# Half of the first weight sums in a Strassen-form down projection, moved from VectorE to a ScalarE copy and an adding transfer

## The chip, the cores and the metric

The kernel runs on one core of a Trainium2 chip, in one launch. The metric is device time in microseconds. A core has five engines with instruction queues of their own, each worked off in order: TensorE (PE in the profile; its weight loads are listed as PEld), VectorE (DVE), ScalarE (ACT), GpSimd (POOL) and SyncE (SP), which here only issues transfers. Sixteen DMA engines carry out the transfers of all queues.

## The reference

One layer of an encoder over 272 positions (16 learned meta tokens and 256 real ones), model width 2048, float32. Two attention groups share one input projection and one output projection; then comes a gated MLP of inner width 5632 with a residual. The part that matters here is its last line, the down projection:

```python
    return (jax.nn.silu(gc) * u) @ w_down      # (256, 5632) @ (5632, 2048), plus the residual h
```

## The kernel before

**Numbers.** Each float32 product is made of three products of a rounded type: every operand is split into a high part and a remainder (hi and lo), and hi x hi, hi x lo and lo x hi are summed in PSUM. For weights, ACT writes the high part (`whi`, listed at its helper's line L238) and DVE subtracts it from the weight to get the remainder (`wlo`, L242). There are four buffers of 1024 columns for whi and four for wlo, in turn. PE gives a pair of buffers back when it has used the piece.

**The down projection.** The 2048 output columns are cut in two. The upper 1024 are made as 8 tiles of 128 columns in the plain way (lines L1870 and L1871 for seven of them, L606 to L608 for the last). The first 1024 are made in the Strassen-Winograd form: with the 256 positions and the 1024 columns each cut in two, 7 block products take the place of 8. They are summed over 22 row pairs; a row pair g is 256 rows of the weight, two blocks of 128, and its four quarters of 128x512 stand side by side in one buffer of 2048 columns, `raw` = [B11 | B12 | B22 | B21] (in the profile `quarters<-in_w_down_s`, two transfers of 512 KB each). These products are at L278; their other operand is either an activation tile (`act`) or sums of activations that were saved to DRAM before and are loaded again (`sin<-s_down`).

The products need four sums of the quarters. `weight_sums` (L529) makes them on DVE in three subtractions, which are called T1, T2 and T3 below:

- T1, 1024 wide: [B12 - B11 | B22 - B12], at the listed L242 as `quarters<-quarters 128x1024`
- T2, 512 wide: B22 - (B12 - B11), and T3, 512 wide: T2's result minus B21, both `quarters<-quarters,quarters 128x512`

A row pair is used in four pieces, each split into whi and wlo like any weight: `raw` columns 1024 to 2047, `raw` columns 0 to 511, the two sums of T1, and the sums of T2 and T3. Pieces of the plain tiles (1024 or 512 columns) stand between them in a fixed order, which `work` (up to L479) writes down; PE takes all pieces in this order.

**Buffers.** There are two buffers of 2048 columns for `raw` (even pairs use one, odd pairs the other) and two for the sums (the same). A `raw` buffer goes back when both of its pieces have been split and T3 is done; then SP may load the pair after next into it.

**What sets the order.** The kernel is written as generator threads; each yields the engine and an assumed cost of its next instruction. The planner (`Flow`, L111) keeps a clock for each engine and always emits the instruction that could start first by these costs. What it emits is each engine's final order; on the chip an engine that must wait holds up all that stand behind it. A load (`load`, L483) is assumed to take its bytes at 350 per ns, in turn, plus 2000 ns. When a plain tile is complete, `down_out` (L1842) has ACT copy it out of PSUM, POOL do three steps on it (L266), and SP store it (`outT`).

Of the kernel before, what the change touches and what calls it, by code (L numbers as in the profile page):

```python
# [11 lines left out]
AF = mybir.ActivationFunctionType  # L12
ALU = mybir.AluOpType
# [192 lines left out]
def encoder_block(ctx: ExitStack, tc: tile.TileContext, io):  # L206
    nc = tc.nc
    ctx.enter_context(tc.manual_schedule())
    fl = Flow()
# [12 lines left out]
    def size(ap):  # L222
        n = 1
        for s in ap.shape[1:]:
            n *= s
        return n

    def in_psum(ap):
        return ap.tensor.name.startswith("bank")

    def columns(*scalars):
        return sum(not (s is None or isinstance(s, float)) for s in scalars)

    def ACT(out, in_, f, **kw):
        ns = (51 if in_psum(in_) else 93) + 0.833 * size(in_)
        ns += 93 * (columns(kw.get("scale")) + columns(kw.get("bias")) > 0)
        yield "act", ns + 113 * ("accum_out" in kw)
        nc.scalar.activation(out, in_, f, **kw)  # L238

    def TT(out, a, b, op):  # L240
        yield "dve", 68 + 1.04 * size(out)
        nc.vector.tensor_tensor(out, a, b, op)  # L242
# [54 lines left out]
    def one(slots):  # L297
        (t,) = yield slots, 1
        return t
# [141 lines left out]
    for w, f in enumerate(QUADS):  # L441
# [6 lines left out]
        for i in range(KC // 2):  # L448
            r = RowPair(io["w_up_s"][w][i], i, PW // 4)
# [18 lines left out]
    for g in range(FC // 2):  # L468
        r = RowPair(io["w_down_s"][g], g, PW // 2)
# [13 lines left out]
    def load(out, src, ev, queue):  # L483
# [4 lines left out]
        queue.dma_start(out, src)  # L488
        fl.set(ev, t + 2000.0 - fl.cur.t)

    n_loads = [0]

    def load_piece():
# [10 lines left out]
    def load_pair(r):  # L504
        if r.of == "up":
            r.raw, r.sums = yield raws, 2
        else:
            r.raw = yield from one(quarters)
        def load_S():
            if r.near:  # L510
                r.ev_S = ev_near[r.g]
                return
            r.S = yield from one(s_parts)
            src, saved = saved_sums[r.of][r.g]
            yield saved
            yield "sp", 600
            load(r.S, src, r.ev_S, nc.sync)

        if r.of == "up":
            yield from load_S()  # L520
        for a in range(0, 4 * r.q, PW):
            yield "sp", 600
            ev = r.loaded if a + PW == 4 * r.q else Event()
            load(r.raw[:, a : a + PW], r.src[:, a : a + PW], ev, nc.sync)
        if r.of == "down":
            yield from load_S()
        fl.spawn(weight_sums(r), (lambda: 0) if r.of == "up" else 2)

    def weight_sums(r):  # L529
        yield r.loaded  # L530
        if r.of == "down":
            r.sums = yield from one(sums4)
        t, raw, q = r.sums, r.raw, r.q
        yield from TT(t[:, : 2 * q], raw[:, q : 3 * q], raw[:, : 2 * q], ALU.subtract)
        fl.set(r.summed[0])
        yield from TT(t[:, 2 * q : 3 * q], raw[:, 2 * q : 3 * q], t[:, :q], ALU.subtract)
        yield from TT(t[:, 3 * q :], t[:, 2 * q : 3 * q], raw[:, 3 * q :], ALU.subtract)
        fl.set(r.summed[1])
        r.used("raw")
# [439 lines left out]
    for h in range(HEADS):  # L979
        t = apool.tile([P, 2, NT], F32R, name=f"ob{h}")  # L980
        ob.append((t[:, 0, :], t[:, 1, :]))
        t = apool.tile([P, 2, NT], F32R, name=f"oa{h}") if h < 6 else hl[KC - HEADS + h]
# [1228 lines left out]
```

## Time and profile before

| what | value |
|---|---|
| runs | 1108.64, 1108.89, 1109.74 us; median 1108.89 us |
| span of the profiled execution | 1106.7 us |
| PE busy in the span | 1100.6 us |
| DVE busy | 990.8 us |
| ACT busy | 735.1 us |
| POOL busy | 140.0 us |
| data moved by DMA | 239.41 MB |
| granted TensorE clock, whole span | 1.000 |

The profile comes from one execution; its own time is its span, from the first to the last instruction, and the runs are timed apart from it, start and end included. Busy shares are averages over stages that are limited by different things, so a stage is looked at by itself. PE's matmuls overlap, and their ends are modelled: how far two starts lie apart says more than how long one is listed. In a listing by groups a row gives line, engine, operation, output and inputs with their shapes and the count, then the total busy time and the mean of one in ns, then the idle time of the engine before these instructions and what ended it. In a timeline a row gives the start, the duration, and the instruction; rows of one kind that follow each other are merged with their count.

### The profile page before, as it was taken

What the parts mean: (1) busy time and instruction counts of PE and PEld (TensorE: products, weight loads), DVE (VectorE), ACT (ScalarE), POOL (GpSimd) and SP (SyncE); (2) the same over time, 40 slices, a digit from 0 to 9 for tenths busy, and PEclk for the clock granted to TensorE, in tenths of its full rate; (3) what the DMA queues carried; (4) which work ended last, traced back from release to release, by engine and by line L of the source; (5) the groups of instructions that cost most, each with busy time, mean ns of one, the idle gap of its engine ahead of it and who ended that gap; (6) DMA issues with size and microseconds to landing.
All of it is one profiled execution on the core that took longest, in us unless ns stands there. A gap on an engine that the chain in (4) does not pass through costs nothing.

```text
span 1106.7 us, 22544 instructions
## 1 busy us (share of the span) xinstructions
PE 1100.6 (99%) x8414; PEld 1061.8 (96%) x8414; DVE 990.8 (90%) x1837; ACT 735.1 (66%) x1470; POOL 140.0 (13%) x202
## 2 busy tenths in 40 slices
PE   9999999999999999999999999999999999999998
PEld 9999999999999999999999999999999988888888
DVE  8979888888878989999999999988988999999984
ACT  8788979798647776656666565665565565655663
POOL 3211222121433400000000000000000011100114
PEclk9999999999999999999999999999999999999999
DMA  9553434444665796657667577777688787777772
GB/s 323 199 172 124 148 127 151 139 163 134 230 188 161 207 343 229 198 181 243 224 193 230 179 248 241 238 229 244 203 275 299 260 299 250 251 258 266 281 249 77
DMA packets 72374, 239.41 MB, mean 216 GB/s; under 512 B 8136, under 2 KB 12744, under 8 KB 72264
## 3 DMA queue, kind: packets, MB, share of 16 engines
q1 hardware_dynamic: 71976, 237.69, 63.8%
q8 instruction: 66, 1.08, 0.4%
q14 instruction: 44, 0.36, 0.1%
q10 hardware_dynamic: 288, 0.27, 0.1%
HBM read 219.44 MB, written 17.83 MB: 214 GB/s over the span
## 4 chain that ended last, share of the span: by engine, by line
PE 90%; ACT 4%; DVE 3%; issue 1%; DMA 1%; POOL 0%; DVEq 0%; POOLq 0%; ACTq 0%
PE bank L278 24%; PE bank L606 18%; PE bank L607 18%; PE bank L608 18%; PE bank L1870 6%; PE bank L1871 3%; PE bank L284 2%; ACT whi L238 1%; ACT scr L238 1%; DVE wlo L242 1%; DVE scr L250 1%; DMA raw<-in_w_cq 1%; ACT qraw L238 0%; ACT bank L238 0%; DVE cols L258 0%
## 5 line engine op out<-in xcount | busy, mean ns | idle before, releaser
L238 ACT ACTIVATE whi<-raw 128x512 fp32r<-128x512 f32 (+2 forms) x479 | 358.1, 764 | 173.2 <-PE bank L607 83.5
L242 DVE TENSOR_TENSOR wlo<-raw,whi 128x512 fp32r<-128x512 f32 (+2 forms) x479 | 414.9, 885 | 43.2 <-ACT whi L238 42.1
L606 PE MATMUL bank<-hl,whi 128*128 128x258 f32 (+2 forms) x1528 | 438.5, 287 | 0.1
L607 PE MATMUL bank<-hl,whi 128*128 128x258 f32 (+2 forms) x1528 | 433.7, 284 | 0.0
L608 PE MATMUL bank<-hl,wlo 128*128 128x258 f32 (+2 forms) x1528 | 433.0, 283 | 0.2 <-DVE wlo L242 0.2
L608 PEld LDWEIGHTS bank<-hl,wlo 128*128 128x128 f32 x1528 | 290.1, 190 | 0.9 <-DVE wlo L242 0.7
L607 PEld LDWEIGHTS bank<-hl,whi 128*128 128x128 f32 x1528 | 289.6, 190 | 0.1
L606 PEld LDWEIGHTS bank<-hl,whi 128*128 128x128 f32 x1528 | 288.6, 189 | 0.5 <-ACT scr L238 0.3
L238 ACT ACTIVATE whi<-quarters 128x1024 fp32r<-128x1024 f32 x88 | 81.5, 950 | 64.8 <-PE bank L1870 46.0
L278 PE MATMUL bank<-whi,act 128*128 128x256 f32 (+1 forms) x420 | 111.5, 317 | 0.0
L1870 PE MATMUL bank<-act,whi 128*128 128x512 f32 x308 | 110.1, 397 | 0.0
L242 DVE TENSOR_TENSOR wlo<-quarters,whi 128x1024 fp32r<-128x1024 f32 x88 | 99.4, 1156 | 10.8 <-ACT whi L238 10.2
L266 POOL TENSOR_TENSOR mt<-mt,mt 128x256 f32<-128x256 f32 x7 | 6.8, 979 | 652.4 <-ACT mt L238 652.4
L1871 PE MATMUL bank<-act,wlo 128*128 128x256 f32 x308 | 86.4, 281 | 0.0
L278 PE MATMUL bank<-whi,sin 128*128 128x512 f32 (+1 forms) x272 | 83.5, 355 | 0.0
L278 PEld LDWEIGHTS bank<-whi,act 128*128 128x128 f32 x420 | 74.1, 189 | 5.7
L1870 PEld LDWEIGHTS bank<-act,whi 128*128 128x128 f32 x308 | 57.8, 188 | 13.9
L278 PE MATMUL bank<-whi,hl 128*128 128x256 f32 x288 | 66.5, 280 | 0.0
L278 PE MATMUL bank<-wlo,act 128*128 128x256 f32 (+1 forms) x210 | 66.3, 315 | 0.0
L238 ACT ACTIVATE whi<-more_raw 128x1024 fp32r<-128x1024 f32 (+2 forms) x46 | 44.1, 962 | 24.4 <-PE bank L607 9.9
L1871 PEld LDWEIGHTS bank<-act,wlo 128*128 128x128 f32 x308 | 58.1, 189 | 1.6
L278 PEld LDWEIGHTS bank<-whi,sin 128*128 128x128 f32 x272 | 49.5, 188 | 7.7
(278 smaller groups left out, 1947.9 us busy)
## 6 DMA issues: line engine op xcount, KB each, us to landing
raw<-in_w_gate SPq DMA_DIRECT2D x83, 512.0 KB, 5.0
raw<-in_w_in SPq DMA_DIRECT2D x52, 512.0 KB, 3.9
raw<-in_w_up_s SPq DMA_DIRECT2D x44, 512.0 KB, 4.9
quarters<-in_w_down_s SPq DMA_DIRECT2D x44, 512.0 KB, 6.9
raw<-in_w_up SPq DMA_DIRECT2D x34, 512.0 KB, 5.5
raw<-in_w_out SPq DMA_DIRECT2D x32, 512.0 KB, 4.0
raw<-in_w_down SPq DMA_DIRECT2D x32, 512.0 KB, 5.2
s_down<-sums SPq DMA_DIRECT2D x22, 512.0 KB, 4.1
```

The source lines that it names most:

```text
L238: nc.scalar.activation(out, in_, f, **kw)
L242: nc.vector.tensor_tensor(out, a, b, op)
L250: nc.vector.scalar_tensor_tensor(out, a, s, b, op0, op1)
L266: nc.gpsimd.tensor_tensor(out, a, b, op)
L278: nc.tensor.matmul(o, l, r, start=start, stop=stop)
L284: nc.tensor.transpose(o, i, ident[:n, :n])
L606: nc.tensor.matmul(ps, whi, xhi, start=start, stop=False)
L607: nc.tensor.matmul(ps, whi, xlo, start=False, stop=False)
L608: nc.tensor.matmul(ps, wlo, xhi, start=False, stop=stop)
L1870: nc.tensor.matmul(ps, whi, x, start=start, stop=False)
L1871: nc.tensor.matmul(ps[:, :n], wlo, x[:, 0, :], start=False, stop=stop)
```

## The change

In the row pairs with an odd number g, 11 of the 22, T1 is made in another way. ACT writes the negative of `raw` columns 0 to 1023 into the buffer of the sums. Then POOL issues a transfer of 128x1024 that adds `raw` columns 512 to 1535 to what stands there. For g = 1, 5, 9, ... the transfer reads its source from the `raw` buffer, for g = 3, 7, 11, ... from the weight in DRAM. T2 and T3 stay on DVE, and DVE waits for the landing ahead of T2. The planner assumes 1000 ns of POOL for the issue and 6000 ns from there to the landing.

```diff
+    def add_dma(out, src, ev):
+        yield "pool", 1000
+        nc.gpsimd.dma_start(out, src, accum_op=ALU.add)
+        fl.cur.t += 6000.0
+        fl.set(ev)
+
...
     def weight_sums(r):
...
         t, raw, q = r.sums, r.raw, r.q
-        yield from TT(t[:, : 2 * q], raw[:, q : 3 * q], raw[:, : 2 * q], ALU.subtract)
+        if r.of == "down" and r.g % 2:
+            yield from ACT(t[:, : 2 * q], raw[:, : 2 * q], AF.Copy, scale=-1.0)
+            src = raw if r.g % 4 == 1 else r.src
+            yield from add_dma(t[:, : 2 * q], src[:, q : 3 * q], Event())
+        else:
+            yield from TT(t[:, : 2 * q], raw[:, q : 3 * q], raw[:, : 2 * q], ALU.subtract)
         fl.set(r.summed[0])
         yield from TT(t[:, 2 * q : 3 * q], raw[:, 2 * q : 3 * q], t[:, :q], ALU.subtract)
         yield from TT(t[:, 3 * q :], t[:, 2 * q : 3 * q], raw[:, 3 * q :], ALU.subtract)
```

Here q is 512. The planner's new costs also move other instructions: the order of PE's instructions is the same in both kernels, DVE's and ACT's orders differ around the 11 pairs (T2 and T3 of an odd pair stand some steps later on DVE than before), POOL has 11 instructions more, and on SP one load and one store change places.

## The prediction

> **What bounds the kernel now.** I read the page first: the share of busy time, then the 40 slices.
>
> ```profile
> PE 1100.6 (99%) x8414; PEld 1061.8 (96%) x8414; DVE 990.8 (90%) x1837; ACT 735.1 (66%) x1470; POOL 140.0 (13%) x202
> ```
>
> PE looks full, but its ends are modelled, so a busy PE proves nothing by itself. The change lies in one stage, the down projection, the last fifth of the span. I therefore asked for a table of windows in that stage, and for its groups by line with the shapes kept apart.
>
> ```profile
> 880.00:900.00 20.00, 20.00 (x100) 16.75 (x99) 19.64 (x23) 14.18 (x19) 3.43 (x3) 1.00 0.70 253
> 1020.00:1040.00 20.00, 20.00 (x100) 16.75 (x99) 19.13 (x19) 13.26 (x16) 3.48 (x3) 1.00 0.88 308
> sum 200.00, PE 200.00 PEld 168.05 DVE 187.72 ACT 118.82 POOL 23.43; mean PE 20.00 PEld 16.81 DVE 18.77 ACT 11.88 POOL 2.34
> ...
> L1870 PE MATMUL bank<-act,whi 128*128 128x512 f32 x273 | 97.7, 397 | 0.0
> L1871 PE MATMUL bank<-act,wlo 128*128 128x256 f32 x273 | 76.6, 280 | 0.0
> L278 PE MATMUL bank<-whi,sin 128*128 128x512 f32 x171 | 60.7, 395 | 0.0
> L278 PE MATMUL bank<-whi,act 128*128 128x512 f32 x130 | 47.6, 394 | 0.0
> L278 PE MATMUL bank<-wlo,sin 128*128 128x512 f32 x85 | 33.4, 393 | 0.0
> L278 PE MATMUL bank<-wlo,act 128*128 128x512 f32 x65 | 25.3, 389 | 0.0
> ```
>
> The columns of a window are its length, then PE, PEld, DVE, ACT and POOL busy, the granted clock, the DMA share and GB/s. The clock is full. To see whether PE really runs without gaps I took the starts of neighbouring matmuls from the timeline:
>
> ```profile
> 904.78 0.40 PE L1870 MATMUL bank<-act,whi 128*128 128x512 f32 x1
> 905.01 0.28 PE L1871 MATMUL bank<-act,wlo 128*128 128x256 f32 x1
> 905.13 0.40 PE L1870 MATMUL bank<-act,whi 128*128 128x512 f32 x1
> ```
>
> A matmul of 512 columns is followed after 0.23 us, one of 256 after 0.12 us (0.232 and 0.118 as medians over the stage's 1213 matmuls). In the 200 us from 880 to 1080 there are 273+171+130+85+65 = 724 wide ones and 273 narrow ones: 724 x 0.232 + 273 x 0.118 = 200.2 us. That is the whole stretch. **PE has no gap in this stage**, so it sets the time; DVE, at 187.7 of 200 us, is close behind but not late. Two more rows say why DVE's load does no harm:
>
> ```profile
> L238 ACT ACTIVATE whi<-quarters 128x1024 fp32r<-128x1024 f32 x65 | 68.7, 1061 | 63.3 <-PE bank L1870 46.0 <-PE bank L278 11.5 <-issue 4.1
> L242 DVE TENSOR_TENSOR wlo<-quarters,whi 128x1024 fp32r<-128x1024 f32 x65 | 81.9, 1269 | 10.8 <-ACT whi L238 10.2
> ```
>
> ACT stands idle until PE frees one of the four whi buffers, DVE until ACT has filled one. Both are held back by PE, not PE by them.
>
> **The change part by part.** In the 11 odd row pairs T1 (the 1024-wide subtraction) leaves DVE:
>
> ```profile
> L242 DVE TENSOR_TENSOR quarters<-quarters 128x1024 f32<-128x1024 f32 x21 | 25.5, 1216 | 0.3 <-DMA quarters<-in_w_down_s 0.3
> L242 DVE TENSOR_TENSOR quarters<-quarters,quarters 128x512 f32<-128x512 f32 x42 | 28.7, 684 | 0.4
> ```
>
> *Removed:* 11 x 1.216 = 13.4 us of DVE. Worth on the path: nothing, since PE has no gap that DVE causes. The order of PE's instructions is the same in both kernels, so its work stays the same.
>
> *Added on ACT:* 11 copies of 128x1024, at 1.06 us (the row above, same shape and engine) 11.7 us. ACT is busy 118.8 of 200 us and idle before its weight copies; that idle time hides them. Without this cover each would push the copies behind it by 1.0 us, and even one of the latest copies is ready 2.2 us before PE uses it (925.61 + 1.06 = 926.67 against 928.87):
>
> ```profile
> 925.61 1.06 ACT L238 ACTIVATE whi<-quarters 128x1024 fp32r<-128x1024 f32 x1 [1.31 <-PE bank L278]
> ...
> 928.87 0.40 PE L278 MATMUL bank<-whi,sin 128*128 128x512 f32 x1
> ```
>
> *Added on POOL:* 11 DMA issues. POOL is busy 23 of 200 us. Each issue waits for ACT's copy; behind it stand the three POOL steps of a finished output tile (L1842), and behind those SP's store of it and SP's next loads. In the stage this happens six times; an issue that is late by less than the 4 to 10 us between it and the next such step moves nothing. Six of the transfers read their source in the loaded buffer, five in DRAM; the trace has rows of neither, and I price both alike.
>
> *Added wait, on the path if anything is:* T2 on DVE now waits for the landing of the adding transfer, and behind T2 stand the wlo subtractions that feed PE. So what counts is L, the time from the end of the negated copy to the landing, against the room that it has. I work out the room for pair 5, the tightest, from the loads, DVE's steps and PE's needs:
>
> ```profile
> 905.95 1.07 SPq L488 DMA_DIRECT2D quarters<-in_w_down_s  x2
> ...
> 905.84 0.68 DVE L242 TENSOR_TENSOR quarters<-quarters,quarters 128x512 f32<-128x512 f32 x1
> 908.91 0.69 DVE L242 TENSOR_TENSOR quarters<-quarters,quarters 128x512 f32<-128x512 f32 x1
> 909.52 2.35 DVE L242 TENSOR_TENSOR wlo<-quarters,whi 128x1024 fp32r<-128x1024 f32 x2
> ...
> 931.90 0.28 PE L1871 MATMUL bank<-act,wlo 128*128 128x256 f32 x1
> ...
> quarters<-in_w_down_s SPq DMA_DIRECT2D x38, 512.0 KB, 6.9
> sin<-s_down SPq DMA_DIRECT2D x20, 512.0 KB, 3.4
> ```
>
> The first row is the load of pair 5 into the buffer of pair 3. In the changed order T2 and T3 of pair 3 stand behind T2 of pair 4 (908.91), so they end about 910.4 instead of 906.5 (905.84 + 0.68), and the second half of the load goes out that much later. It lands 6.9 us on, at 917.4 or a little later; the negated copy ends at about 918.9. On the other side, behind T2 of pair 5 the new order has T3, two wlo of 1024, T1 of pair 6 and one more wlo of 1024, which PE needs at 931.90. From start to start a T step takes 0.61 us (908.91 to 909.52) and a wide one 1.14 (two take 2.35): 2 x 0.61 + 3 x 1.14 + 1.22 = 5.9. T2 must start by 925.9 at the latest. **Room of pair 5: 925.9 - 918.9 = 7.0 us.** The same arithmetic gives 7.8 us for pair 9 and 8.6 to 11.0 us for the other nine.
>
> Now L. The trace of before has no adding transfer and no DMA issued by POOL. From below: 3.4 us, the same 512 KB alone in the queue (sin). From above: the transfer has to read the destination as well as the source, so twice the slowest landing of a weight load of this stage (8.7 us): 17.4 us.
>
> ```profile
> DMA to landing us min/median/max: 2.0/6.8/8.7
> ```
>
> I take 6.9 us, the median load of the same size in the same traffic, and 1.0 us for POOL's issue, between SP's own issue (half of the 1.07 us for two) and the longest POOL step of an output tile (1.60 us, quoted with the rivals): L = 7.9 us. Then pair 5 is late by 0.9 us, pair 9 by 0.1, the rest not. **Sum: +1.0 us.** The profiled execution spans 1106.7 us; the median of the runs is 1108.89 us, 2.2 us more, which lies outside the span and which I leave as it is. Forecast: 1108.9 + 1.0 = 1109.9 us.
>
> The Trainium skill gives a price for a DMA issued by GpSimd: on the page "DMA: Bandwidth & Descriptors", section "Anatomy of one DMA — SWDGE (gpsimd) path", about 2.0 us plus the bytes by 436 GB/s. For 512 KB that is an estimate of 3.2 us, and by it no pair would be late and the time would be 1108.9 us. The trace's own loads beside other traffic (6.9 us) go against taking it here.
>
> **A second bound: the turn of the buffer.** All odd pairs share one buffer for the loaded quarters. Pair 5's load is issued at 905.95, pair 21's at 1056.22:
>
> ```profile
> 1056.22 0.96 SPq L488 DMA_DIRECT2D quarters<-in_w_down_s  x2
> ```
>
> That is 8 turns in 150.3 us, 18.8 us each. In the new kernel a turn holds the load (6.9), the negated copy (1.06), L, and T2 with T3 (1.3): 9.3 + L. With L = 7.9 it is 17.2 us and fits. From L = 9.5 us on, every further us costs one us in each of about 10 turns.
>
> **The rivals.**
>
> *The adding transfer is slow (slower; chance 0.33).* Its price is the turn: at L = 11 us, 1.5 us x 10 = 15 us, 1124 us; at L = 13.8 us (twice the median load), 43 us, 1152 us. It decides from L = 9.5 us. For it: both operands have to be read; and POOL and DVE hold each other up, as the wlo below shows (1.70 us beside a POOL step, 1.21 us without one). If POOL's issue is held up in the same way, each DVE instruction of 1.2 us that it has to sit out adds as much to L, and with DVE at 94% busy three of them make 11.5 us. Against it: a good part of the 6.9 us of a plain load is queueing behind its own first half.
>
> ```profile
> 896.68 1.70 DVE L242 TENSOR_TENSOR wlo<-raw,whi 128x1024 fp32r<-128x1024 f32 x1
> 897.38 1.60 POOL L266 TENSOR_TENSOR mt<-mt,res 128x256 f32<-128x256 f32 x1
> 901.12 1.21 DVE L242 TENSOR_TENSOR wlo<-raw,whi 128x1024 fp32r<-128x1024 f32 x1
> ```
>
> The Trainium skill, "SBUF — State Buffer", section "SBUF: two separate sides", states such a hold-up: while VectorE runs in a two-port mode, GpSimd cannot write the descriptors of its DMA. Whether DVE's two-input subtractions do this no run here shows yet, since POOL issues no DMA in the trace of before.
>
> *The loads become late (slower; 0.15).* The DMA share is 0.70 and 0.88 in the two windows quoted. Eleven transfers of 0.5 MB, counted one to three times over for two reads and one write, are 5.8 to 17.3 MB on top of the stage's traffic of about 250 GB/s x 220 us = 55 MB, 10 to 31% more. If the landing of a load grows by the same 31%, to 9.0 us, the turn with L = 7.9 is 19.3 us, 0.5 us too long: with pair 5's 0.9 about 6 us, 1115 us. It decides from a landing of 8.5 us. Against it: most loads wait in buffers for some us before use.
>
> *DVE was the limit after all (faster; 0.03).* Then up to 13.4 us would come back, 1095.5 us. PE's spacing speaks against it.
>
> **How the numbers follow.** A measurement of this kernel can tell about 0.2%, 2.2 us, from no change. The forecast, full or nearly full cover (L up to about 8.5 us: +0 to +2 us, 1108.5 to 1111 us), has 0.47. Slower by the add 0.33, by the loads 0.15, and 0.02 for a wait that I have not named; faster 0.03. The likeliest single case is the forecast, though slower has a little more in all. The range goes from 1107.8 (the forecast's lower end less 0.7 us, since the runs of before lie up to 0.85 us from their median) to 1128 us: it leaves out the faster case, and of the slow add the part with L over 11.4 us, about 0.15.
>
> **What would show it.** Right: PE's spacing stays 0.232 and 0.118 us through the stage, the T1 group falls from 22 to 11, DVE's busy time in 880 to 1080 falls by about 12 us, ACT's rises by about 11, the adding transfers land within 8 us, DVE waits for them under 1 us each. Wrong: idle time of DVE's 128x512 T steps, or of ACT's whi copies, ended by a DMA; PE idle ended by wlo in odd pairs only; or weight loads that land later than 7 us in the median. A time under 1106 us would mean that PE had gaps that I did not see.

## The result, and the profile after

| what | before | after |
|---|---|---|
| median of the runs | 1108.89 us | 1117.71 us (1116.45, 1117.71, 1119.66) |
| ratio after / before | | 1.0081, 95% interval 1.0067 to 1.0095 |
| span of the profiled execution | 1106.7 us | 1117.9 us |

The change costs 8.8 us by the medians; the forecast was +1.0 us. The profiled execution of after is the slowest of its three runs and lies 11.2 us above that of before. First the page of after: the busy times, the queues, and the chain that ended last. q1 carries SP's loads, q0 the new transfers.

```profile
PE 1104.4 (99%) x8414; PEld 1062.4 (95%) x8414; DVE 980.8 (88%) x1826; ACT 744.7 (67%) x1481; POOL 150.2 (13%) x213
...
q1 hardware_dynamic: 71976, 237.69, 62.0%
q0 software_dynamic: 1584, 5.77, 2.7%
...
PE 79%; DVE 7%; DMA 7%; ACT 4%; issue 2%; POOL 0%; SPq 0%; DVEq 0%; ACTq 0%; POOLq 0%
```

The same chain in the page of before:

```profile
PE 90%; ACT 4%; DVE 3%; issue 1%; DMA 1%; POOL 0%; DVEq 0%; POOLq 0%; ACTq 0%
```

DVE is relieved by 10.0 us and ACT loaded by 9.6, as intended, and PE executes the same 8414 matmuls. But the chain of waits, 90% PE before, now goes through DVE and DMA for 7% each. The table of windows over the same 200 us as before shows where:

```profile
900.00:920.00 20.00, 17.84 (x83) 14.60 (x82) 14.86 (x16) 9.37 (x11) 0.87 (x1) 0.91 0.77 252
920.00:940.00 20.00, 18.68 (x93) 15.43 (x92) 15.44 (x15) 11.94 (x15) 5.21 (x4) 1.00 0.87 269
960.00:980.00 20.00, 19.46 (x97) 16.13 (x96) 16.18 (x17) 12.72 (x15) 5.25 (x5) 1.00 1.01 342
...
sum 200.00, PE 193.04 PEld 159.70 DVE 169.09 ACT 121.30 POOL 32.69; mean PE 19.30 PEld 15.97 DVE 16.91 ACT 12.13 POOL 3.27
```

PE, busy for 200.00 us there before, now has 193.04. From start to start of neighbouring matmuls, against the medians of 0.232 and 0.118 us that still hold, seven stalls over 0.3 us lie in the stage: 2.35 us at 912.6, 1.47 at 936.1, 0.70 at 972.6, 1.18 at 1011.3, 0.39 at 1050.4, 0.37 at 1067.6, 1.75 at 1070.9, together 8.2. With the slow restarts behind them the excess from 880 to 1090 is 10.8 us (before: 0.2), nearly the whole difference of the spans. The groups of the same 200 us, with the idle time before each behind the bar:

```profile
L238 ACT ACTIVATE whi<-quarters 128x1024 fp32r<-128x1024 f32 x62 | 65.3, 1059 | 66.0 <-PE bank L1881 28.9 <-DMA quarters<-quarters 13.2 <-DMA quarters<-in_w_down_s 7.5
L242 DVE TENSOR_TENSOR quarters<-quarters,quarters 128x512 f32<-128x512 f32 x40 | 27.4, 690 | 8.2 <-DMA quarters<-quarters 5.8 <-DMA quarters<-in_w_down_s 1.7
L242 DVE TENSOR_TENSOR quarters<-quarters 128x1024 f32<-128x1024 f32 x10 | 13.3, 1331 | 6.0 <-DMA quarters<-in_w_down_s 6.0
L493 POOL DMA_DIRECT2D quarters<-quarters x5 | 4.4, 872 | 60.2 <-DVE wlo L242 36.4 <-ACT quarters L238 18.9 <-DMA sin<-s_down 4.7
```

And the issues from 880 to 1090 (count, KB, median us to landing):

```profile
quarters<-in_w_down_s SPq DMA_DIRECT2D x38, 512.0 KB, 7.2
quarters<-in_w_down_s POOLq DMA_DIRECT2D x5, 512.0 KB, 8.7
quarters<-quarters POOLq DMA_DIRECT2D x5, 512.0 KB, 9.5
```

Before, no idle time of ACT ahead of these copies was put down to a DMA; now 20.7 us are. Two waits appear on DVE: T2 and T3 for the adding transfers (8.2 us in all), and the T1 that stayed on DVE, that of the even pairs, for a plain load (6.0 us). These are the two rivals of the prediction side by side: the slow add, and the loads that become late. (The name `quarters<-in_w_down_s` stands both for SP's loads and for the adding transfers with their source in DRAM.)

The longest stall, 2.35 us at 912.6, stands behind a late load. DVE's rows ahead of it:

```profile
910.69 1.23 DVE L242 TENSOR_TENSOR quarters<-quarters 128x1024 f32<-128x1024 f32 x1 [3.30 <-DMA quarters<-in_w_down_s]
911.95 2.02 DVE L242 TENSOR_TENSOR quarters<-quarters,quarters 128x512 f32<-128x512 f32 x3
```

T1 of pair 4 waits 3.30 us for a load of SP. The three short steps behind it are T2 of pair 4 and T2 and T3 of pair 3, whose added sums had landed at 911.28. By the last DMA that DVE waited for, this stall and the one at 1050.4 belong to the loads, together 4.4 us with the slow restart; the other five stand behind a T2 that waited for its transfer.

One pair followed through, pair 5, in the timeline of after (ACT, POOL, DVE and PE rows; the rest left out):

```profile
920.54 1.04 ACT L238 ACTIVATE quarters<-quarters 128x1024 f32<-128x1024 f32 x1
...
921.88 0.86 POOL L493 DMA_DIRECT2D quarters<-quarters  x1 [18.94 <-ACT quarters L238]
...
930.55 1.42 DVE L242 TENSOR_TENSOR quarters<-quarters,quarters 128x512 f32<-128x512 f32 x2 [0.47 <-DMA quarters<-quarters]
...
931.89 2.52 DVE L242 TENSOR_TENSOR wlo<-quarters,whi 128x1024 fp32r<-128x1024 f32 x2
...
934.33 1.77 DVE L242 TENSOR_TENSOR quarters<-quarters 128x1024 f32<-128x1024 f32 x1
...
935.10 1.60 POOL L266 TENSOR_TENSOR mt<-mt,s 128x256 f32<-128x256 f32 x1
936.02 1.75 DVE L242 TENSOR_TENSOR wlo<-raw,whi 128x1024 fp32r<-128x1024 f32 x1
...
937.83 0.39 PE L1882 MATMUL bank<-act,wlo 128*128 128x256 f32 x1 [1.32 <-DVE wlo L242]
```

The negated copy ends at 921.58, POOL issues 0.3 us later, the transfer lands at 930.53: L = 8.9 us. T2 and T3 follow at once, then two wlo, T1 of pair 6 and the wlo that PE waits for. That order is the one the prediction worked with. Of the 1.47 us that PE loses, DVE's wait for the transfer makes only 0.47; the run with one partition, below, shows the rest. Over the eleven odd pairs L is 7.1 to 11.0 us, 9.0 in the median.

**Why L is 9 us.** The transfer of pair 3, ahead of the dip at 912.6, has the answer. It is issued at 902.07, 1.7 us after SP began to issue two loads of an even pair. The queues, from the issue to the first packet of q0, and from there to the landing (packets, MB, share of 16 engines):

```profile
q1 hardware_dynamic: 338, 1.20, 87.4%
```

```profile
q0 software_dynamic: 144, 0.52, 52.3%
q1 hardware_dynamic: 280, 1.02, 51.5%
```

For 4.2 us (902.0 to 906.2) the sixteen engines work on loads and not one packet of the adding transfer moves; for the next 5.1 us the two queues share the engines. So L is 0.3 us to the issue, 4.2 to the first packet, 4.7 of packets beside the loads, 0.3 to the landing. The medians of the eleven are alike: 4.3 us to the first packet, landing 8.65 us after the issue. In nine of the eleven SP had issued a load in the last 2.2 us or did so 0.3 us later, and the first packet took 3.4 to 5.6 us; in the other two (875.6, 1017.9) it took 1.6. That the loads are what the first packet waits for is read from this; no run takes the loads away. A load that shares the engines pays too: the second half of the even pair, issued at 900.82, landed 9.8 us later.

### The profile page after: what moved, and what is told of

Its sections match the earlier page's. It is cut to its first block, busy times and chain, and to the rows that moved or that the text cites. A ratio compares the mean times of both kernels' runs of the same rounds, so it can differ in the third digit from the quotient of the medians.

```text
span 1117.9 us, 22582 instructions
## 1 busy us (share of the span) xinstructions
PE 1104.4 (99%) x8414; PEld 1062.4 (95%) x8414; DVE 980.8 (88%) x1826; ACT 744.7 (67%) x1481; POOL 150.2 (13%) x213
## 4 chain that ended last, share of the span: by engine, by line
PE 79%; DVE 7%; DMA 7%; ACT 4%; issue 2%; POOL 0%; SPq 0%; DVEq 0%; ACTq 0%; POOLq 0%
PE bank L278 19%; PE bank L617 18%; PE bank L618 18%; PE bank L619 18%; PE bank L1881 4%; DVE wlo L242 3%; DMA quarters<-quarters 3%; PE bank L284 2%; PE bank L1882 2%; DMA quarters<-in_w_down_s 2%; ACT whi L238 2%; DVE quarters L242 1%; DMA s_up<-sums 1%; DVE scr L250 1%; DMA raw<-in_w_cq 1%
## 5 line engine op out<-in xcount | busy, mean ns | idle before, releaser
L493 POOL DMA_DIRECT2D quarters<-quarters x6 | 5.4, 898 | 548.8 <-ACT quarters L238 507.6
```

What stands on the lines that cost most here:

```text
L493: nc.gpsimd.dma_start(out, src, accum_op=ALU.add)
```

## The experiments

All times are medians, run beside the kernel before on the same chip; ratios are to it, with their 95% interval. The order of PE's instructions is the same in all fourteen kernels. DVE, ACT and SP have the order of after in three of the runs: the plain transfer, the one partition, and the one partition twice. L means, as in the prediction, from the end of the negated copy to the moment its sum is there.

### The copy without the transfer

One run keeps the copy and drops the transfer:

```diff
             yield from ACT(t[:, : 2 * q], raw[:, : 2 * q], AF.Copy, scale=-1.0)
-            src = raw if r.g % 4 == 1 else r.src
-            yield from add_dma(t[:, : 2 * q], src[:, q : 3 * q], Event())
```

> ScalarE still writes the negated copy in the eleven odd pairs, but nothing is added to it, so their weight sums lack a term (q2 and q1 are never added): that leaves DVE without its eleven T1 of 1.22 us and TensorE without any wait for a transfer. Both theories (the wait for the adding transfer itself; its traffic beside the even pairs' loads) expect the time of before, 1108.0 to 1110.0 us, and TensorE's stalls of the down stage at most 1 us in sum. A third theory, that ScalarE's eleven copies of 1.04 us or the moved instruction order cost the time, expects 1114 to 1118 us.

Measured: 1109.11 us, ratio 1.0002 (0.9993 to 1.0012). The row of its windows:

```profile
sum 200.00, PE 199.97 PEld 167.60 DVE 176.93 ACT 127.84 POOL 24.00; mean PE 20.00 PEld 16.76 DVE 17.69 ACT 12.78 POOL 2.40
```

DVE is down by 10.8 us and PE's 200 us don't move: the relief was worth nothing, as predicted, and the copies cost nothing. The third theory falls for the copies only: without the assumed landing the planner gives DVE another order here than in after, so this run doesn't test that order (the run with one partition does). This is also the bound of the idea: with DVE's work gone and not even a transfer in its place, nothing is gained.

### The transfer without adding

```diff
-        nc.gpsimd.dma_start(out, src, accum_op=ALU.add)
+        nc.gpsimd.dma_start(out, src)
```

> The same transfers in the same places, but they overwrite instead of adding (the negated copy is lost, the sums of the odd pairs lack that term). The kernel after showed 2.74 us of transfer time on each DMA engine for an adding transfer against 1.46 for a load of the same bytes. If the length comes from the adding, landing after the copy's end falls from a median of 9.0 us to about 7.2, the median of the plain loads, and the time to 1110 to 1113 us. If it comes from the issue on GpSimd and from the crowd on the DMA engines, landing stays at 8.5 to 9 and the time at 1115 to 1119.

Measured: 1112.12 us, ratio 1.0026 (1.0016 to 1.0036); L 7.6 us in the median, 7.3 from issue to landing. Its queues from 880 to 1090, and those of after:

```profile
q0 software_dynamic: 1445, 5.26, 6.5%
```

```profile
q0 software_dynamic: 1468, 5.29, 13.2%
```

About the same packets and bytes take half the engines' time: a 4 KB packet 0.16 us instead of 0.33. Adding doubles the price of the bytes and puts 1.4 us on L, and without both the time is 5.6 us lower. Of the 3.3 us that stay, about 1.8 are lost even when next to nothing is carried (the run with one partition).

### The traffic without the wait

VectorE makes every sum as before; ten odd pairs (all but g = 1) also make the copy and the adding transfer, into a buffer that nobody reads:

```diff
+    def unused_sums(r):
+        q = r.q
+        s = yield from one(combined)
+        yield from ACT(s, r.raw[:, : 2 * q], AF.Copy, scale=-1.0)
+        src = r.raw if r.g % 4 == 1 else r.src
+        yield from add_dma(s, src[:, q : 3 * q], Event())
+        fl.put(combined, s)
...
+        if r.of == "down" and r.g % 2:
+            if r.g > 1:
+                fl.spawn(unused_sums(r), 2)
```

> VectorE makes all sums as before; beside it ten of the odd pairs also make the negated copy and the adding transfer, into a buffer that nobody reads (work in addition, no term of the result is touched). Only traffic and ScalarE's copy are left, no wait on the sums. If the wait for the transfer carries the loss: 1108.5 to 1110.5 us. If the even pairs' loads, pushed out by the traffic to 9 to 11 us, carry it: 1113 to 1118 us, and TensorE's stalls stand behind T1 sums of even pairs that waited for a load.

Measured: 1114.72 us, ratio 1.0049 (1.0032 to 1.0066). Five of these transfers hold a raw buffer as their source, so the next run reads DRAM in all ten (`src = r.src`):

> As the run with sums that nobody waits for (1114.7 us), but the source is always DRAM, so that no transfer holds a raw buffer: there five of the ten read the raw buffer and kept it for their own length. If the traffic on the DMA engines alone makes the even pairs' loads late, the time stays at 1112 to 1116 us; if the held raw buffer did it, the time falls to 1108.5 to 1110.5.

Measured: 1113.27 us, ratio 1.0036 (1.0023 to 1.0049). The two intervals overlap; the held buffer is no large part. Their control keeps the copy into the unread buffer, and their order on PE, DVE, ACT and SP, and leaves out the transfer:

> The control of the two runs whose sums nobody waits for (1114.7 and 1113.3 us): ScalarE's negated copy into the unread buffer stays, in the same place and with the same order on TensorE, VectorE, ScalarE and SyncE, and the transfer goes. If the transfer's traffic made those runs slower: 1108.5 to 1110 us. If ScalarE's added copy did, by putting the weight splits behind it off by 1.05 us each time: 1112 to 1115 us.

Measured: 1108.78 us, ratio 1.0002 (0.9992 to 1.0011). T1 on DVE in the run with DRAM sources, and in the control:

```profile
L242 DVE TENSOR_TENSOR quarters<-quarters 128x1024 f32<-128x1024 f32 x21 | 25.6, 1220 | 10.3 <-DMA quarters<-in_w_down_s 10.3
```

```profile
L242 DVE TENSOR_TENSOR quarters<-quarters 128x1024 f32<-128x1024 f32 x21 | 25.5, 1215 | 1.1 <-DMA quarters<-in_w_down_s 1.0
```

T1 waits ten times as long for plain loads as without the traffic. So the traffic alone, with nobody waiting for it, costs 4.4 to 5.9 us.

### The wait without the traffic

The kernel after, but each transfer carries one partition of 128:

```diff
-            yield from add_dma(t[:, : 2 * q], src[:, q : 3 * q], Event())
+            yield from add_dma(t[:1, : 2 * q], src[:1, q : 3 * q], Event())
```

> The order of every engine is that of the kernel after, but the adding transfer carries one partition of 128 (4 KB; in the odd pairs the other partitions' sums lack q1 and q2). It waits behind the loads in the queues as the full one does (first packet 4.3 us after the issue in the median of the kernel after) and then has one packet instead of 4.3 us of them: landing is estimated at 5 us. Wait theory: L of 5 to 5.5 us is inside every room, 1108.5 to 1110.5. Traffic theory: nothing is carried, also 1108.5 to 1110.5. If the order of the instructions alone costs what the kernel after lost, 1114 or more.

Measured: 1110.81 us, ratio 1.0016 (1.0007 to 1.0026), a little above both theories. L is 5.9 us: 4 KB wait 4.0 us for their first packet just as 512 KB do. Two stalls of 0.92 us are left, in pairs 5 and 19. They are not the wait for the transfer. In the 200 us DVE stands idle ahead of T2 and T3 for 0.7 us in all, none of it put down to a DMA, and in pair 5 T2 starts 1.3 us after the landing (924.34):

```profile
923.88 1.83 DVE L242 TENSOR_TENSOR wlo<-quarters,whi 128x1024 fp32r<-128x1024 f32 x2 [1.51 <-ACT whi L238]
925.62 1.42 DVE L242 TENSOR_TENSOR quarters<-quarters,quarters 128x512 f32<-128x512 f32 x2
926.96 2.52 DVE L242 TENSOR_TENSOR wlo<-quarters,whi 128x1024 fp32r<-128x1024 f32 x2
929.39 1.77 DVE L242 TENSOR_TENSOR quarters<-quarters 128x1024 f32<-128x1024 f32 x1
931.09 1.75 DVE L242 TENSOR_TENSOR wlo<-raw,whi 128x1024 fp32r<-128x1024 f32 x1
```

In its new place T2 stands behind two wlo steps that had to wait for whi, so it couldn't start earlier, however fast the transfer. From there to the end of the needed wlo it takes 7.2 us, as in after, and PE is late. So these 1.8 us, all that the run loses, come from the order that the change gives DVE, with POOL's steps running beside T1 and the last wlo; in the run with the copy alone, where T2 stands elsewhere, no stall over 0.3 us is left.

Then two such transfers in a chain (the second `dma_start` repeated behind the first):

> As the run with one small transfer, but two of them in a chain, the second one issued when the first has landed: from 5 us each, L is estimated at 8.5 to 11 us with next to no bytes. This is the wait without the traffic. If the wait alone carries the loss, 1115 to 1120 us; if the loss needs the traffic, 1108.5 to 1111; if the two share it (traffic without a wait gave 4.4 to 5.9 us of 8.8), 1111 to 1114.

Measured: 1119.16 us, ratio 1.0095 (1.0078 to 1.0112), with L 9.06 us in the median, 7.0 to 11.6. The groups of this run for T2 and T3, and for POOL's second issue:

```profile
L242 DVE TENSOR_TENSOR quarters<-quarters,quarters 128x512 f32<-128x512 f32 x40 | 28.6, 716 | 14.0 <-DMA quarters<-in_w_down_s 9.4 <-DMA quarters<-quarters 4.0
...
L494 POOL DMA_DIRECT2D quarters<-in_w_down_s x5 | 3.8, 764 | 25.6 <-DMA quarters<-in_w_down_s 25.6
```

With next to no bytes (q0 has 0.6% of the engines there, and the loads land in 6.4 us) the wait, in the order of after, gives the whole loss. The traced execution took 1122.80 us, the other three 1118.7 to 1119.4. Two things make it a little harder than the wait of after: L is spread wider, and POOL itself stands still until the first transfer has landed, 5 us in each pair.

### Half the bytes

ACT and the transfer make only the first sum of T1; DVE makes the second:

```diff
-            yield from ACT(t[:, : 2 * q], raw[:, : 2 * q], AF.Copy, scale=-1.0)
+            yield from ACT(t[:, :q], raw[:, :q], AF.Copy, scale=-1.0)
             src = raw if r.g % 4 == 1 else r.src
-            yield from add_dma(t[:, : 2 * q], src[:, q : 3 * q], Event())
+            yield from add_dma(t[:, :q], src[:, q : 2 * q], Event())
+            yield from TT(t[:, q : 2 * q], raw[:, 2 * q : 3 * q], raw[:, q : 2 * q], ALU.subtract)
```

> Only the first of the two sums is made by the adding transfer (256 KB), the second by VectorE (a 128x512 subtract, about 0.7 us, that T3 needs but T2 doesn't). Bytes and landing shrink together: about 6.5 us in place of 9.0. Wait and traffic theory both expect 1109 to 1112 us, with the traffic theory at the upper end; if a fixed cost of the software-queue transfer (issue, write order) carries the loss it stays at 1115 or more.

Measured: 1117.86 us, ratio 1.0083 (1.0068 to 1.0098): no better than after, above both theories and in the range of the third, a cost that doesn't shrink with the bytes. L is 9.0 us again; from 880 to 1090:

```profile
q0 software_dynamic: 1440, 2.62, 6.9%
...
quarters<-in_w_down_s POOLq DMA_DIRECT2D x5, 256.0 KB, 8.0
quarters<-quarters POOLq DMA_DIRECT2D x5, 256.0 KB, 8.9
```

Half the bytes take half the engines' time and land hardly earlier. What goes ahead of the first packet (4.7 us) and the sharing behind it set L, not the bytes. The planner put the second sum (0.74 us in the mean) just ahead of T2; in five of the eleven pairs DVE starts it after the landing, so that T2 comes later than L alone would have it, in the other six before. In the next run the subtraction stands ahead of the transfer:

> As the run with half the bytes (1117.9 us, where VectorE's second sum stood behind the assumed landing and came between it and T2), but VectorE's 128x512 subtract now stands ahead of the transfer in the plan. L stays near 9 us (half the bytes landed no earlier), the traffic is half of the kernel after. If the wait alone counts: 1115 to 1118 us; if the traffic counts too: 1112 to 1115.

Measured: 1114.31 us, ratio 1.0043 (1.0028 to 1.0058). It lies where the traffic theory put it, but L came out at 8.4 us rather than 9 and DVE's order is another, so this run alone doesn't separate the two.

### The add on GpSimd

```diff
-            yield from add_dma(t[:, : 2 * q], src[:, q : 3 * q], Event())
+            yield from PTT(t[:, : 2 * q], raw[:, q : 3 * q], t[:, : 2 * q], ALU.add)
```

> GpSimd adds q2 and q1 to the negated copy itself (one 128x1024 add) instead of issuing the transfer: the wait on the second engine stays, the traffic goes. From GpSimd's 128x256 adds of 0.97 to 1.38 us in the kernel after, one such add is estimated at 3.9 to 5.5 us, well inside the smallest room of 7.0 us. Both theories expect 1108 to 1111 us; only a third one, that any sum made off VectorE loses by the waits and the moved order, expects 1114 or more.

Measured: 1111.75 us, ratio 1.0026 (1.0016 to 1.0036), between the two ranges, although L is 2.9 us and no DMA is added. Its groups:

```profile
L242 DVE TENSOR_TENSOR wlo<-quarters,whi 128x1024 fp32r<-128x1024 f32 x63 | 89.9, 1442 | 10.4 <-ACT whi L238 10.3
L266 POOL TENSOR_TENSOR quarters<-quarters,quarters 128x1024 f32<-128x1024 f32 x11 | 34.4, 3130 | 578.1 <-ACT quarters L238 567.6 <-DVE quarters L242 10.5
```

DVE's wide subtractions beside it take 1.44 us in the mean instead of 1.27: 63 x 0.17 = 10.7 us, so DVE gets back nearly all that it gave away, and gets it in the stretches behind a negated copy. That this is what costs the 2.9 us is argued from the rows; it wasn't tried apart.

### Where the planner puts T2

Only the assumed landing, `fl.cur.t += 6000.0` in `add_dma`, is changed: to 9000 and to 3000.

> Only the planner's assumed landing of the adding transfer is raised from 6.0 to 9.0 us, near the measured median of 9.0, so that T2 and T3 are placed later on VectorE behind work that is ready. If T2 holds up ready work on VectorE because it stands too early in its order, the time falls to 1110 to 1115 us. If the pieces of the pair itself are what TensorE waits for, nothing is gained: 1116 to 1119 us.

> Only the planner's assumed landing is lowered from 6.0 to 3.0 us, so T2 and T3 stand earlier on VectorE; raising it to 9.0 gave 1131.8 us. If a T2 that stands early is only late by its own transfer and what is queued behind it has room, 1115 to 1119 us; if VectorE then waits at T2 with ready work behind it, 1122 to 1135 us.

Measured: 1131.76 us (ratio 1.0199, 1.0169 to 1.0228) with 9000, outside both ranges, and 1136.42 us (1.0258, 1.0231 to 1.0285) with 3000, just above the second one. T2 and T3 with 3000, then with 9000:

```profile
L242 DVE TENSOR_TENSOR quarters<-quarters,quarters 128x512 f32<-128x512 f32 x38 | 26.2, 689 | 37.9 <-DMA quarters<-in_w_down_s 19.5 <-DMA quarters<-quarters 17.8
```

```profile
L242 DVE TENSOR_TENSOR quarters<-quarters,quarters 128x512 f32<-128x512 f32 x39 | 28.3, 738 | 0.8
L242 DVE TENSOR_TENSOR quarters<-quarters 128x1024 f32<-128x1024 f32 x10 | 12.2, 1222 | 8.1 <-DMA quarters<-in_w_down_s 8.1
L238 ACT ACTIVATE whi<-quarters 128x1024 fp32r<-128x1024 f32 x59 | 62.1, 1058 | 65.7 <-PE bank L1881 26.9 <-DVE quarters L242 12.8 <-DMA quarters<-quarters 11.7
```

At 3000 DVE stands for 37.9 us before T2 with ready work behind it: in all eleven pairs the step behind T2 or T3 starts with no further wait. At 9000 it no longer waits, but T2 and T3 come after work that isn't ready either: ACT waits 12.8 us for the sums, and the buffers go back later. Neither value plans the wait away; 6000 is the best of the three, and no others were run.

### The runs by L

| run | L, median us | q0's share, 880 to 1090 | ratio |
|---|---|---|---|
| control: unread copy, no transfer | none waited for | 0 | 1.0002 |
| copy alone | none | 0 | 1.0002 |
| one partition | 5.9 | 0.3% | 1.0016 |
| plain transfer | 7.6 | 6.5% | 1.0026 |
| half the bytes, sum ahead | 8.4 | 6.9% | 1.0043 |
| after | 9.0 | 13.2% | 1.0081 |
| half the bytes, sum behind | 9.0 | 6.9% | 1.0083 |
| one partition, twice | 9.06 | 0.6% | 1.0095 |
| add on GpSimd (DVE slowed beside it) | 2.9 | 0 | 1.0026 |
| unread sums, DRAM source | none waited for | 12.8% | 1.0036 |
| unread sums | none waited for | 12.6% | 1.0049 |

The two runs with another assumed landing are left out; their L of 9.6 (3000) and 10.1 us (9000) go with other orders. Four runs differ in the transfer alone: one partition, the plain transfer, after, and one partition twice. In them the ratio rises with L whatever the bytes are, and so does DVE's idle time ahead of T2 and T3 in the 200 us: 0.7, 2.6, 8.2 and 14.0 us. At L = 9 the runs with 13.2% and 0.6% have overlapping intervals. The first of the four loses nothing to the wait; its 1.8 us are the order's, and the other three have that order too. Without a wait the bytes still cost half to two thirds of the loss. The two don't add up (4.4 to 5.9 and about 10 us, against 8.8 together): both make sums late for the same PE deadlines, and PE stalls for the later one. In the one traced execution of after the stalls behind late loads make 4.4 of the 10.8 us lost; how the 8.8 us divide can't be said more closely than this.

## Where the prediction was right, and where it was wrong

**Right.** PE had no gap, its order stayed, and DVE's relief is worth nothing (1.0002). ACT's copies are hidden (1.0002). The wait ahead of T2 is on the path, and the sum was to be made of L against a room. The rival of the slow add named the place, and the rival of the loads the other half. T1's group fell from 21 to 10 in the 200 us.

**Luck.** The measured 1117.71 us lies inside the range, 1107.8 to 1128, but not by the forecast case: +1.0 us was forecast, +8.8 came. The range reached that far for the slow add, priced by the turn of the raw buffer from L = 9.5 on, and that is not how the time was lost. The signs that the prediction named for being wrong came: T2 and ACT's copies waited for DMAs, and the median load took 7.2 us, over its limit of 7.

**The step that failed** is the size of L: "6.9 us, the median load of the same size in the same traffic, and 1.0 us for POOL's issue, ...: L = 7.9 us". Measured: 9.0 us in the median. The issue was dear enough at 1.0 (0.3 us from the copy's end to the issue); the landing took 8.65 from there instead of 6.9. The price of a load was the wrong neighbour for two reasons that the runs take apart: an adding packet takes 0.33 us instead of 0.16 (plain copy: L 7.6, 5.6 us less time), and the transfer is issued just behind loads of the other pair and gets its first packet only after 4.3 us (one partition: 4.0 us for 4 KB).

**The rooms were too wide as well.** The size of L alone doesn't make 8.8 us: by the prediction's own rooms, L = 9.0 is 2.0 us too long for pair 5, 1.2 for pair 9 and at most 0.4 for each of the other nine, 3.2 to 6.8 us in all. And at L = 7.6, under the forecast's 7.9, the plain copy still lost 3.3 us and not at most 1.0. Pair 5 shows why. From T2 to the end of the needed wlo the prediction allowed 5.9 us; in the timeline of after it is 930.55 to 937.77, 7.2 us. T1 of pair 6 took 1.77 us instead of 1.22 and the wlo behind it 1.75 instead of 1.14, because POOL's three steps of an output tile ran beside them (the middle one is in the timeline above, 935.10). The rows that show this hold-up stood in the prediction, among the rivals, and weren't carried into the room. With 7.2 us in place of 5.9, T2 of pair 5 would have had to start 1.3 us earlier than the room's latest start, and in the run with one partition DVE's new order didn't let it start in time even with the sum already there. The same holds for pair 19, to which the prediction gave 8.6 us or more. Late T2 steps of the new order were counted for pair 3's buffer, but not as a cost by themselves.

**The rivals.** The slow add was to decide from L = 9.5 by the turn of the raw buffer. The time was lost earlier: after lost 8.8 us at L = 9.0, by PE's deadlines, pair by pair; only pairs 3, 9, 13, 19 and 21 had L over 9.5. The turn grew with the stalls (negated copy of pair 5 to that of pair 21: 156.0 us for 8 turns, 19.5 each, against 18.8). Nor was a plain load's landing mostly queueing behind its own first half, as was held against this rival: in before the halves issued at 926.31 and 926.73 landed after 6.15 and 6.99 us. The loads were to grow to 9.0 us; their median went from 6.9 to 7.2 only, and it was 7.1 in the control without any such transfer. What grew were single loads that an adding transfer ran beside: 9.8 us at 900.82, 10.4 at 960.54, 10.8 at 998.39 and 9.6 at 1038.88, where the slowest before took 8.7. T1 waited for the first of them (3.30 us) and the last (1.00 us). A median hid them.

**The two places cited.** By the Trainium skill, page "DMA: Bandwidth & Descriptors", section "Anatomy of one DMA — SWDGE (gpsimd) path", a transfer of 512 KB was an estimate of 3.2 us. The shortest that ran here took 5.4 us without adding and 6.6 with it, and the median in after was 8.65; the measurement decides against it. The hold-up that the Trainium skill, page "SBUF — State Buffer", describes in "SBUF: two separate sides", VectorE in a two-port mode keeping GpSimd from writing descriptors, didn't show: the first packet came after 1.6 us in the two cases with no load issued close by, and DVE was busy for the whole of these 1.6 us. Whether its subtractions run in such a mode no run shows.

## What to carry to other kernels

Price a transfer that something waits for by what stands ahead of it at the moment of its issue, not by the median of other transfers: here half of 9 us was spent behind loads, and neither half the bytes (4.7 us to the first packet) nor a 128th of them (4.0) shortened that part by much. Where one event (a buffer that comes free) triggers both a load and the work that leads to a transfer, the two meet every time, and each makes the other late. An engine at 94% that the bottleneck never waits for has nothing to give: moving its work into a longer chain trades idle time that cost nothing for latency that does. A planner's new assumption moves other work too: a run in which the transfer carries next to nothing shows what the new order costs by itself, here 1.8 us.

## What the runs showed of the hardware

Adding doubled the DMA engines' time: 13.2% against 6.5% for about the same bytes and packets.

A stall of TensorE can cost more than its length. Windows of after around the longest one (clock in the third column from the end):

```profile
912.00:914.00 2.00, 1.00 (x6) 0.57 (x4) 1.97 (x4) 0.45 (x1) 0.00 (x0) 1.00 0.88 353
914.00:916.00 2.00, 0.84 (x3) 0.65 (x4) 1.93 (x2) 1.91 (x3) 0.00 (x0) 0.86 0.46 152
916.00:918.00 2.00, 2.00 (x6) 1.62 (x5) 2.00 (x3) 1.56 (x3) 0.00 (x0) 0.50 0.37 147
918.00:920.00 2.00, 2.00 (x9) 1.60 (x9) 1.88 (x3) 0.43 (x1) 0.00 (x0) 0.79 0.16 23
920.00:922.00 2.00, 2.00 (x13) 1.76 (x12) 1.23 (x1) 1.58 (x2) 0.12 (x1) 1.00 0.90 358
```

After 2.35 us lost by one matmul the granted clock fell to 0.50, and matmuls of 512 columns followed each other after 0.43 us; that put 1.7 us on top of the stall. The length alone doesn't decide: with the landing assumed at 9000 three stalls of 2.2 to 2.6 us cost another 1.6 to 2.3 us each; with 3000 one of 3.3 us cost another 1.6, and four of 2.5 to 3.0 us no more than 0.5 us each. Nothing here shows what else it hangs on.
